# A triangular inversion's input copied in two parts, by two engines: three quarters one pair of heads earlier, one quarter where all of it was

## The chip, the cores and the metric

The kernel runs on one core of a Trainium2 chip. A core has engines that each work through a queue of their own, in order: TensorE (PE: matmuls, and PEld, the loads of their stationary operand), VectorE (DVE), ScalarE (ACT), GpSimd (POOL) and SyncE (SP, which here issues DMA transfers). They meet through semaphores. Data lie in SBUF (128 partitions), matmul results in PSUM. The metric is the device time of one execution in microseconds, as the median of several runs; lower is better. Beside it stands a profile of one execution, in which every instruction has a start, a duration and, where its engine idled, what ended the idle time.

## The reference

Two residual layers over 512 tokens with 1024 features, in float32. Each has a token mixer and a gated ConvFFN. The second layer's mixer is RWKV-7, and its heart is a recurrence over time for 16 heads of 64:

```python
def step(state, inp):
    r_t, w_t, k_t, v_t, a_t, b_t = inp
    sa = jnp.einsum('bhvk,bhk->bhv', state, a_t)
    state = (state * w_t[:, :, None, :]
             + sa[..., None] * b_t[:, :, None, :]
             + v_t[..., None] * k_t[:, :, None, :])
    y_t = jnp.einsum('bhvk,bhk->bhv', state, r_t)
    return state, y_t
```

Around it stand projections of the token-shifted input (r, k, v and low-rank ones for decay, a and gate), a normalization of each head, a bonus term and an output projection. The change touches only how one intermediate of this recurrence is prepared; what is computed stays the same.

## The kernel before

The kernel does the recurrence in chunks of 64 tokens (8 chunks). Within a chunk the steps depend on each other through a 64x64 lower triangular matrix per head and chunk, I minus a strictly triangular part, and the kernel inverts it. Two heads make a **pair**, which fills the 128 partitions; there are 8 pairs, four in each of two **groups** g. The strictly triangular parts of a group lie in the tile `ti[g]` (4 pairs x 8 chunks = 32 units of 64 columns), and the inverse replaces them in place.

`rwkv_main` is made of Python generators. Each `yield` ends a step, and what a step traces goes to the framework.

- `pairs()` is the main line. For pair p it runs `decay` (of pair p + 2: tanh, a scan along time at L911, exponentials, the squares at L913 that the matmul at L923 sums), `operands` (of pair p + 1: products on VectorE) and `products` (of pair p), in three steps. `products` has two halves of four chunks; each multiplies on PE (L973), masks on VectorE (L977, tile `lq`) and lets ScalarE copy the triangular part into `ti` (L978). After the third step p goes into the set `done`. The test runs when the generator is resumed, so a condition such as "3 in done" is first seen after the first step of the next pair.
- `fill` is a chain of generators that keep PE busy: dense projections for k and v (L325 to L327, three matmuls per product: high and low parts), the value path (`value`: L868, L873, L883, L885), then gates and the output projection. `value` uses the PSUM tag `mm`, which has two banks in turn, as the projections do. A bank is free for the next projection when its reader is done; L885 on VectorE is such a reader.
- `invert(g)` is the side line. It takes the two 32x32 diagonal blocks of every 64x64 matrix (`Q`: four sets of 32 partitions and 32 columns) out of `ti[g]` into the tile `ix` (L1041 to L1046), turns every 32x32 block over on VectorE (`turn`, L1051, into tile `li`), sets the diagonal to one (L1055) and then runs a chain of 60 small VectorE instructions (L1062 to L1070), each of which needs the one before. At the end come two more turns (L1051) and matmuls with copies for the block beside the diagonal (L1090 to L1105). For g = 0 the four copies into `ix` are all ScalarE's, of 32 units x 32 columns = 1024 elements each. For g = 1 they are cut already: 24 units on ScalarE, a yield, the last 8 units on VectorE.
- `weave(main, side, fill, rate, lag, side_rate)` interleaves them: per step of the main line so many steps of `fill` and of `side`.

The lines that set where the first inversion starts:

```python
self.weave(until(main, lambda: 3 in done), None, fill, *RATES[0], ktiles=STEPS[0])
inv = invert(0)
for _ in take(inv, FIRST0):
    pass
self.weave(until(main, lambda: KT - 2 in done), inv, fill, *RATES[1], ktiles=STEPS[1])
```

With `FIRST0` = 1, `take` runs `invert(0)` up to its first yield: the copies, the first turn, the diagonal.

The order in an engine's queue is not exactly the order of tracing. The framework plans it when the program is built: among the instructions whose inputs are ready by its own estimate of times it takes the one traced first. A later traced instruction can thus go into a gap that the planner sees. `tc.issue_after(x)` only demands that what is traced under it comes behind x on x's engine. Semaphores follow from the tiles that an instruction reads and writes.

Of the kernel before, what the change touches and what calls it, by code (L numbers as in the profile page):

```python
# [32 lines left out]
RATES = ((1.9, 2), (1.9, 6, 2.2), (0.66, 2, 1.15), (0.72, 2), (1.2, 6, 2.2))  # L33
LEAD = 1
WB = 4
FIRST0, WAIT, STEPS = 1, 1, (2, 2, 2, 2)
# [108 lines left out]
class Emit:  # L145
# [622 lines left out]
    def rwkv_main(self, r, ctx, gain):  # L768
# [22 lines left out]
        ks, used, done, vdone = {}, set(), set(), set()  # L791
# [203 lines left out]
        def pairs():  # L995

            units = [type("Unit", (), {})() for _ in range(KT)]

            def start(p):
                if p >= KT:  # L1000
                    return iter(())
                while p not in ks:
                    next(fill)
                if p == 0:
                    second_factors(p)
                return decay(p, units[p])

            yield from start(0)
            nxt = start(1)
            operands(0, units[0])  # L1010
            for _ in nxt:
                yield
            for p in range(KT):
                nxt = start(p + 2)
                if p + 1 < KT:
                    operands(p + 1, units[p + 1])
                parts = products(p, units[p])
                for n in range(3):
                    next(nxt, None)
                    with ExitStack() as behind:  # L1020
                        if n < 2:
                            behind.enter_context(tc.issue_after(self.last(mybir.EngineType.PE)))
                        next(parts, None)
                    yield
                done.add(p)

        def invert(g):

            tg = ti[g].rearrange("p i c t -> p (i c) t")
            Q = [(slice(64 * hd + 32 * b, 64 * hd + 32 * b + 32), slice(32 * b, 32 * b + 32))
                 for hd in range(2) for b in range(2)]

            def blocks(tag):
                return ip.tile([P, 32, 32], F32, tag=tag, bufs=1 if tag == "off" else 2, name=self.uid(tag))

            x = blocks("ix")
            pr = ip.tile([P, 272], F32, tag="pr", bufs=1, name=self.uid("pr"))
            cut = 24 * g  # L1040
            for us in (slice(0, cut), slice(cut, 32))[1 - g:]:  # L1041
                for rows, cols in Q:
                    if us.start and g == 1:
                        V.tensor_copy(x[rows, us], tg[rows, us, cols])
                    else:
                        S.copy(x[rows, us], tg[rows, us, cols])  # L1046
                if g == 1 and us.start == 0:
                    yield
            def turn(out, src):
                for bs in [slice(n, n + 8) for n in range(0, 32, 8)] if g == 1 else [slice(0, 32)]:  # L1050
                    V.transpose(out[:, bs], src[:, bs])  # L1051

            tt = blocks("li")
            turn(tt.rearrange("p s t -> p t s"), x.rearrange("p u t -> p t u"))
            V.memset(tt.rearrange("p s t -> p (s t)")[:, 0:1024:33], 1.0)  # L1055
            for _ in range(WAIT):
                yield
            for j in range(1, 31):
                ni = 31 - j
                to = tt[:, 0:j, j + 1:32]  # L1060
                if j == 1:
                    V.scalar_tensor_tensor(to[:, 0], tt[:, 1, 2:32], tt[:, 0, 1:2], to[:, 0], ALU.mult, ALU.add)  # L1062
                elif ni == 1:
                    V.scalar_tensor_tensor(to[:, :, 0], tt[:, 0:j, j], tt[:, j, 31:32], to[:, :, 0], ALU.mult, ALU.add)
                else:
                    a = tt[:, j, j + 1:32].unsqueeze(1).to_broadcast([P, j, ni])
                    b = tt[:, 0:j, j].unsqueeze(2).to_broadcast([P, j, ni])
                    q = pr[:, 0:ni * j].rearrange("p (c i) -> p c i", i=ni)
                    V.tensor_tensor(q, a, b, ALU.mult)
                    V.tensor_tensor(to, to, q, ALU.add)  # L1070
                if j % 2 == 1:
                    yield

            z, y = blocks("ix"), blocks("li")
            turn(z.rearrange("p u t -> p t u"), tt)
            if g == 0:
                next(fill)
            turn(y.rearrange("p u t -> p t u"), tt.rearrange("p s t -> p t s"))
            yield
            off, own = blocks("off"), iter(Q)  # L1080
            for i in range(2):
                for hf in range(2):
                    ps = self.acc("aux" if g == 1 else "e").rearrange("p (u t) -> p u t", t=32)
                    us = slice(16 * hf, 16 * hf + 16)
                    for u in range(16):
                        for hd in range(2):
                            b0, b1 = Q[2 * hd][0], Q[2 * hd + 1][0]
                            n = 16 * hf + u
                            if i == 0:
                                nc.tensor.matmul(ps[b1, u, :], tg[b0, n, 32:64], z[b0, n, :], start=True, stop=True,  # L1090
                                                 tile_position=(b0.start, b1.start))
                            else:
                                nc.tensor.matmul(ps[b0, u, :], off[b1, n, :], y[b1, n, :], start=True, stop=True,
                                                 tile_position=(b1.start, b0.start))
                        if u % 8 == 7:
                            if i == 0:
                                rows, cols = next(own)
                                S.copy(tg[rows, :, cols], y[rows])
                            yield
                    for hd in range(2):  # L1100
                        b0, b1 = Q[2 * hd][0], Q[2 * hd + 1][0]
                        if i == 0:
                            S.copy(off[b1, us], ps[b1])
                        else:
                            S.copy(tg[b0, us, 32:64], ps[b0])  # L1105
# [277 lines left out]
        def project():  # L1383

            for g in range(2):
                while g not in gated:
                    yield
                for m in range(2 - 2 * g, KT):
                    if m % 2 == 0:
                        w = wo.take()  # L1390
                    a = self.acc("mm")
                    yield from self.dense_steps(a, w, outs[g], c0=m % 2 * 512)
                    with ExitStack() as behind:
                        if left is None:
                            behind.enter_context(tc.issue_after(self.last(mybir.EngineType.DVE)))
                        V.tensor_tensor(self.h[m], self.h[m], a, ALU.add)
                    if g == 1:
                        self.absorb(m, gain)
# [7 lines left out]
        def take(gen, n):  # L1406
            for _ in range(n):
                if next(gen, self) is self:
                    return
                yield  # L1410

        def until(gen, end):
            for _ in gen:
                yield
                if end():
                    return


        fill = itertools.chain(projections(), gates(), project())
        gw, ga = {}, {}  # L1420
        main = pairs()
        self.weave(until(main, lambda: 3 in done), None, fill, *RATES[0], ktiles=STEPS[0])
        inv = invert(0)
        for _ in take(inv, FIRST0):
            pass
        self.weave(until(main, lambda: KT - 2 in done), inv, fill, *RATES[1], ktiles=STEPS[1])
        load(0, 0)
        ahead = invert(1)
        next(ahead)
        self.weave(main, inv, fill, *RATES[4], ktiles=STEPS[1])  # L1430
# [5 lines left out]
        inv = ahead  # L1436
# [88 lines left out]
```

## Time and profile before

| what | us |
|---|---|
| runs (3) | 1244.2, 1244.65, 1246.1 |
| median | 1244.65 |
| the profiled execution | 1245.55 |
| its span in the profile | 1243.7 |
| first copy into `ix` for group 0 starts (L1046) | 650.96 |
| first turn of group 0 starts (L1051) | 656.56 |
| last small instruction of its chain ends (L1064) | 697.64 |

The difference between the profiled execution's time and its span, 1.85 us, lies outside the profile. Times in rows are from the span's start. A row of the timeline reads: start, duration, engine, line of the source, operation, tile written <- tiles read, shape and count, and in brackets the idle time of the engine before it and what ended that. Durations of neighbours can overlap by some 0.1 us, since an engine starts the next instruction before the last has left it.

### The profile page before, as it was taken

To read this page: it belongs to the slowest core of one execution; us is meant where nothing else is said; L and a number is where in the kernel's file an instruction comes from. 1 tells how busy PE (TensorE), PEld (TensorE's weight loads), DVE (VectorE), ACT (ScalarE), POOL (GpSimd) and SP (SyncE) were. 2 spreads that over 40 slices of the span, in tenths; PEclk is the share of its full clock that TensorE was granted. 3 is DMA by queue.
4 is the path that set the end of the run, shared out by engine and by line. 5 is a ranking of instruction groups with operands and counts; after the bars stand their busy time and mean duration, and the time that the engine had idled before them with its cause. 6 is when DMAs were issued, how large, how long until landed. Compare 5 with 4: busy or idle time off the path is not lost.

```text
span 1243.7 us, 19411 instructions
## 1 busy us (share of the span) xinstructions
PE 1226.8 (99%) x7535; PEld 1000.2 (80%) x7535; DVE 851.1 (68%) x1418; ACT 633.1 (51%) x1089; POOL 81.4 (7%) x106
## 2 busy tenths in 40 slices
PE   9999999999999999999999999999999999999997
PEld 6878888888888888877887777778888888888886
DVE  5566578888876454675899698776777777872323
ACT  6544455555554343466787667424544444543232
POOL 1100200000000001000000013222000000000000
PEclk9999999999999999999999899999999999999999
DMA  7232457887556776326888797654223223333332
GB/s 273 94 105 82 132 180 246 246 249 241 192 172 193 220 226 196 109 81 182 220 242 237 188 280 233 219 171 135 85 102 102 90 97 102 97 88 104 97 93 81
DMA packets 125133, 201.65 MB, mean 162 GB/s; under 512 B 39857, under 2 KB 63153, under 8 KB 125041
## 3 DMA queue, kind: packets, MB, share of 16 engines
q10 hardware_dynamic: 38976, 112.87, 29.5%
q1 hardware_dynamic: 86064, 87.54, 22.6%
q8 instruction: 59, 0.97, 0.3%
q14 instruction: 34, 0.27, 0.1%
HBM read 152.93 MB, written 47.45 MB: 161 GB/s over the span
## 4 chain that ended last, share of the span: by engine, by line
PE 91%; DVE 4%; DMA 3%; ACT 1%; issue 0%; SPq 0%; POOL 0%; DVEq 0%; POOLq 0%; ACTq 0%
PE mm L325 9%; PE mm L327 9%; PE mm L326 9%; PE aux L325 6%; PE aux L326 6%; PE aux L327 6%; PE e L325 6%; PE e L326 6%; PE us L325 6%; PE e L327 6%; PE us L327 6%; PE us L326 6%; PE us L1314 1%; PE aux L973 1%; PE aux L988 1%; PE us L1321 1%
## 5 line engine op out<-in xcount | busy, mean ns | idle before, releaser
L237 ACT CAST w<-w 128x512 fp32r<-128x512 f32 x340 | 206.5, 611 | 359.8 <-PE aux L327 92.6
L238 DVE TENSOR_TENSOR w<-w,w 128x512 fp32r<-128x512 f32 x340 | 230.5, 680 | 180.2 <-ACT w L237 179.6
L325 PE MATMUL mm<-mxh,w 128*128 128x512 f32 x408 | 167.9, 412 | 2.7 <-DVE rt L885 2.6
L327 PE MATMUL mm<-mxh,w 128*128 128x512 f32 x408 | 161.1, 395 | 0.0
L326 PE MATMUL mm<-mxl,w 128*128 128x512 f32 x408 | 160.6, 394 | 0.0
L325 PEld LDWEIGHTS mm<-mxh,w 128*128 128x128 f32 x408 | 77.0, 189 | 22.8 <-DVE rt L885 3.3
L327 PEld LDWEIGHTS mm<-mxh,w 128*128 128x128 f32 x408 | 77.0, 189 | 17.1 <-issue 0.8
L326 PEld LDWEIGHTS mm<-mxl,w 128*128 128x128 f32 x408 | 77.1, 189 | 16.2 <-issue 1.7
L575 ACT ACTIVATE cv<-z,par 128x512 f32<-128x512 f32 x88 | 71.7, 817 | 26.5 <-DVE z L573 21.2
L325 PE MATMUL aux<-mxh,w 128*128 128x512 f32 x216 | 84.5, 391 | 0.0
L325 PE MATMUL us<-mxh,w 128*128 128x512 f32 x216 | 84.5, 391 | 0.0
L327 PE MATMUL aux<-mxh,w 128*128 128x512 f32 x216 | 84.2, 390 | 0.0
L326 PE MATMUL aux<-mxl,w 128*128 128x512 f32 x216 | 84.1, 389 | 0.0
L326 PE MATMUL us<-mxl,w 128*128 128x512 f32 x216 | 84.1, 389 | 0.0
L327 PE MATMUL us<-mxh,w 128*128 128x512 f32 x216 | 84.1, 389 | 0.0
L354 POOL TENSOR_TENSOR ss<-ss,sq 128x512 f32<-128x512 f32 x24 | 31.7, 1323 | 761.1 <-ACT sq L352 761.1
L325 PE MATMUL e<-mxh,w 128*128 128x512 f32 x208 | 81.4, 391 | 0.0
L326 PE MATMUL e<-mxl,w 128*128 128x512 f32 x208 | 81.1, 390 | 0.0
L327 PE MATMUL e<-mxh,w 128*128 128x512 f32 x208 | 81.0, 389 | 0.0
L576 DVE SCALAR_TENSOR_TENSOR cv<-z,par,cv 128x512 f32<-128x512 f32 x88 | 66.0, 752 | 19.5 <-ACT cv L575 19.5
L577 DVE SCALAR_TENSOR_TENSOR cv<-z,par,cv 128x512 f32<-128x512 f32 x88 | 66.0, 752 | 2.9
L325 PEld LDWEIGHTS aux<-mxh,w 128*128 128x128 f32 x216 | 40.5, 188 | 9.0 <-issue 0.5
(1113 smaller groups left out, 2555.2 us busy)
## 6 DMA issues: line engine op xcount, KB each, us to landing
w<-in_wup ACTq DMA_DIRECT2D x88, 512.0 KB, 3.7
w<-in_wdn ACTq DMA_DIRECT2D x32, 512.0 KB, 3.7
st<-std SPq DMA_DIRECT2D x15, 640.0 KB, 6.6
w<-wkd ACTq DMA_DIRECT2D x16, 512.0 KB, 5.1
w<-wvd ACTq DMA_DIRECT2D x16, 512.0 KB, 5.1
w<-wod ACTq DMA_DIRECT2D x16, 512.0 KB, 4.2
w<-in_wdn ACTq DMA_DIRECT2D x16, 384.0 KB, 3.3
w<-in_wsu ACTq DMA_DIRECT2D x8, 512.0 KB, 3.7
```

The costliest lines, as they stand in the source:

```text
L237: nc.scalar.copy(hi[r, :n], src)
L238: (lo_eng or nc.vector).tensor_tensor(lo[r, :n], src, hi[r, :n].bitcast(F32), ALU.subtract)
L325: mm(acc, wh, xh, start=first, stop=False)
L326: mm(acc, wh, xl, start=False, stop=False)
L327: mm(acc, wl, xh, start=False, stop=last)
L354: nc.gpsimd.tensor_tensor(self.ss, self.ss, self.sq, ALU.add)
L575: nc.scalar.activation(c, z[:, 2:], AF.Identity, scale=cw(2, i), bias=self.p("conv_b", l * 44 + i))
L576: nc.vector.scalar_tensor_tensor(c, z[:, 1:T + 1], cw(1, i), c, ALU.mult, ALU.add)
L577: nc.vector.scalar_tensor_tensor(c, z[:, 0:T], cw(0, i), c, ALU.mult, ALU.add)
L973: nc.tensor.matmul(qs[hd][:, c - ch.start, :], bk[H[hd], c, C * hd:C * hd + P], ar[H[hd], c, :], start=True, stop=True)
L988: nc.tensor.matmul(qs[hd][:, c, :], bk[H[hd], c, C * hd:C * hd + P], dg[H[hd], c, :], start=True, stop=True)
L1314: nc.tensor.matmul((us, ux)[hd][H[hd], 1, i, :], ti[g][H[hd], i, c, :], wt[H[hd], i, :], start=True, stop=True)
```

## The change

`invert(g)` cuts its copies for both groups alike: four copies of units 0 to 23 on ScalarE, a yield, four copies of units 24 to 31 on VectorE. The generator `invert(0)` is made before the first `weave`. A wrapper, `opened`, stands around the main line there: at the first step after pair 2 (the third) is done, it runs `invert(0)` up to its new first yield, so that the ScalarE copies of the first three pairs' 24 units are traced behind the first step of pair 3. The call of `take` after the `weave` then runs the step that follows: the VectorE copies of the fourth pair's 8 units, the first turn and the diagonal. Later steps of the inversion are traced where they were.

```diff
-            cut = 24 * g
-            for us in (slice(0, cut), slice(cut, 32))[1 - g:]:
+            for us in (slice(0, 24), slice(24, 32)):
                 for rows, cols in Q:
-                    if us.start and g == 1:
+                    if us.start:
                         V.tensor_copy(x[rows, us], tg[rows, us, cols])
                     else:
                         S.copy(x[rows, us], tg[rows, us, cols])
-                if g == 1 and us.start == 0:
+                if us.start == 0:
                     yield
...
-        self.weave(until(main, lambda: 3 in done), None, fill, *RATES[0], ktiles=STEPS[0])
         inv = invert(0)
+
+        def opened(gen):
+            for _ in gen:
+                if 2 in done and not begun:
+                    begun.append(next(inv))
+                yield
+
+        begun = []
+        self.weave(opened(until(main, lambda: 3 in done)), None, fill, *RATES[0], ktiles=STEPS[0])
         for _ in take(inv, FIRST0):
             pass
```

## The prediction

> **What bounds the kernel now.** I read the page first, for the engine that never rests.
>
> ```profile
> span 1243.7 us, 19411 instructions
> ...
> PE 1226.8 (99%) x7535; PEld 1000.2 (80%) x7535; DVE 851.1 (68%) x1418; ACT 633.1 (51%) x1089; POOL 81.4 (7%) x106
> ```
>
> TensorE (PE) is busy for 1226.8 of 1243.7 us. A change that removes no matmul can win only what PE loses by waiting, 16.9 us in all, and what it loses by running at less than its full clock. So the next view is the busy time of each engine in stretches of 10 us around the code that is changed (columns: busy us and count of PE, weight loads, VectorE (DVE), ScalarE (ACT), GpSimd; then the granted PE clock, DMA share, GB/s).
>
> ```profile
> 630.00:640.00 10.00, 10.00 (x57) 8.09 (x56) 9.94 (x18) 7.86 (x15) 0.00 (x0) 1.00 0.66 182
> 640.00:650.00 10.00, 10.00 (x107) 8.46 (x106) 8.80 (x17) 7.49 (x16) 0.11 (x1) 1.00 0.80 236
> 650.00:660.00 10.00, 9.34 (x66) 7.74 (x68) 7.06 (x16) 8.71 (x14) 0.00 (x0) 1.00 0.89 238
> 660.00:670.00 10.00, 9.44 (x82) 7.37 (x81) 9.93 (x22) 7.68 (x15) 0.11 (x1) 1.00 0.79 206
> 670.00:680.00 10.00, 10.00 (x98) 8.61 (x98) 9.93 (x25) 7.32 (x17) 0.00 (x0) 1.00 0.93 246
> 680.00:690.00 10.00, 9.65 (x82) 7.51 (x82) 9.76 (x23) 4.51 (x10) 0.61 (x2) 1.00 1.03 283
> 690.00:700.00 10.00, 7.53 (x48) 5.43 (x48) 9.52 (x24) 4.21 (x8) 0.00 (x0) 0.90 0.87 246
> 700.00:710.00 10.00, 10.00 (x133) 8.09 (x129) 3.15 (x4) 6.17 (x11) 0.00 (x0) 0.76 0.39 105
> ```
>
> Three things are to be seen. Up to 650 PE is never idle. From 660 to 700 VectorE is, at 9.5 to 9.9 of 10, so in that stage it is as much the bound as PE is. And PE pays twice near 695: it idles for 2.47 us in 690 to 700, and the granted clock falls to 0.90 and then 0.76, which is 1.0 + 2.4 = 3.4 us of full-speed work lost. The view of what PE waited for, 650 to 700, names the waits:
>
> ```profile
> PE mm L325 <- DVE rt L885: 2.6, 2, 2.3
> PE e L923 <- ACT sq L913: 0.7, 1, 0.7
> PE e L899 <- DVE kn L950: 0.6, 1, 0.6
> ```
>
> One wait is on ScalarE (0.7 us), the rest on a late VectorE. Why VectorE is late shows where the first inversion begins. The timeline of ScalarE, then that of VectorE:
>
> ```profile
> 650.96 1.04 ACT L1046 COPY ix<-ti 32x1024 f32<-32x1024 f32 x1
> 652.01 0.62 ACT L957 COPY bk<-bk 64x512 f32<-64x512 f32 x1
> 652.63 1.05 ACT L1046 COPY ix<-ti 32x1024 f32<-32x1024 f32 x1
> 653.70 0.41 ACT L978 COPY ti<-lq 64x256 f32<-64x256 f32 x1
> 654.12 1.04 ACT L1046 COPY ix<-ti 32x1024 f32<-32x1024 f32 x1
> 655.07 0.40 ACT L978 COPY ti<-lq 64x256 f32<-64x256 f32 x1
> 655.48 1.05 ACT L1046 COPY ix<-ti 32x1024 f32<-32x1024 f32 x1
> 656.55 0.63 ACT L913 ACTIVATE sq<-kn 128x512 f32<-128x512 f32 x1
> ```
>
> ```profile
> 652.57 1.22 DVE L911 TENSOR_TENSOR_SCAN sq<-cst,sq 128x512 f32<-128x512 f32 x1
> 656.56 2.02 DVE L1051 STREAM_TRANSPOSE li<-ix 128x1024 f32<-128x1024 f32 x1 [2.77 <-ACT ix L1046]
> ```
>
> VectorE stands at the transpose for 2.77 us until the fourth copy is done; the same copies hold L913 back, for which PE waits. The four copies were traced one after another, yet other instructions stand between them: the order in a queue is the framework's plan and not that of the source. I come back to this.
>
> **The change part by part.** It splits the four copies of 1024 elements into four of 768 on ScalarE, traced after the first half of the fourth pair, and four of 256 on VectorE where all four stood. The second inversion (g = 1) already has this form, so the trace has both prices. VectorE's row and ScalarE's:
>
> ```profile
> 714.75 1.18 DVE L1044 COPY ix<-ti 32x256 f32<-32x256 f32 x4
> ```
>
> ```profile
> 711.77 2.51 ACT L1046 COPY ix<-ti 32x768 f32<-32x768 f32 x3
> ```
>
> *VectorE.* It gains the 2.77 us of waiting and pays 1.18 us for four copies. They come in behind the scan that ends at 652.57 + 1.22 = 653.79, so the transpose would begin near 654.97 and not at 656.56: **1.6 us earlier**. Two reasons could make it less. The instructions behind the transpose wait for L923, which gets only 0.7 us earlier; the copies could also be planned into VectorE's idle time before, which would make it more (at most 2.77).
>
> *ScalarE before 650.* Three copies take 2.51 us, so four take 2.51 / 3 x 4 = 3.3 us. Their last input is the third pair's second half, and from 630 to 650 ScalarE idles 2.14 + 2.51 = 4.65 us by the table above. This holds them, but in pieces:
>
> ```profile
> ACT sq L906 <- PE e L901: 1.7, 1, 1.7
> ACT mt L690 <- DVE mxl L238: 1.0, 1, 1.0
> ```
>
> (That view is ScalarE's waits from 628 to 650, the two longest.) Only these two pieces hold a copy of 0.84 us whole. What queues behind a misplaced copy is the pair's own chain, above all the square L913 that PE's L923 reads. Its slack there:
>
> ```profile
> 640.05 0.63 ACT L913 ACTIVATE sq<-kn 128x512 f32<-128x512 f32 x1
> ```
>
> ```profile
> 641.64 1.05 PE L923 MATMUL e<-cst,sq 128*128 128x128 f32 x8
> ```
>
> L913 ends at 640.68, 0.96 us before PE wants it. One copy ahead of it costs nothing; two cost 2 x 0.84 - 0.96 = 0.7 us of PE; four would cost 2.4 us. I take nothing, because PE has 10.00 of 10 busy there with filling matmuls and 1.7 us of the gaps lie behind L913; 0 to 2.4 us goes into the range.
>
> *ScalarE after 650.* 4.2 us of copies go away, so L913 is no longer held and PE's 0.67 us before L923 go. No DMA, PSUM bank or SP instruction is added, and ScalarE's weight loads (issued from its queue) move with it by about a microsecond at most, none of which PE is seen to wait for here. The number of steps per turn of the interleaving loop is unchanged, since one extra step is used up early.
>
> *The sum.* From 656.56 to 697 VectorE is busy for 9.5 to 9.9 of every 10 us and waits for no other engine for long, so if its order stays, everything it does there is 1.6 us earlier, and so is the end of PE's last wait. The two timelines at this place (PE, then VectorE):
>
> ```profile
> 692.30 1.02 PE L883 MATMUL mm<-rt,wb 128*128 128x512 f32 x2
> ...
> 696.99 0.50 PE L325 MATMUL mm<-mxh,w 128*128 128x512 f32 x1 [2.28 <-DVE rt L885]
> ```
>
> ```profile
> 696.25 0.68 DVE L885 TENSOR_TENSOR rt<-mm,v 128x512 f32<-128x512 f32 x1
> ...
> 697.67 1.99 DVE L1051 STREAM_TRANSPOSE ix<-li 128x1024 f32<-128x1024 f32 x1
> 699.51 1.97 DVE L1051 STREAM_TRANSPOSE li<-li 128x1024 f32<-128x1024 f32 x1
> ```
>
> PE's small waits are used up first: 0.67 (gone with the copies), 0.6 (L950) and about 0.3 (the other L885, 2.6 - 2.3) make 1.6 us. PE thus arrives at the last wait 1.6 us earlier, VectorE's L885 comes 1.6 us earlier too, and the wait stays about **2.2 us** long. With it stays the clock's fall behind it. What is late next is the same L885. So the gain is 1.6 us and not 1.6 + 2.28 + 3.4. Behind 700 PE is the bound again and carries the shift on. Against the profiled execution's own 1245.55 us (span 1243.7 and 1.85 around it) this gives 1243.95; the median of the runs is 0.9 lower, 1244.65, and from it the forecast is 1244.65 - 1.6 = **1243.05 us**.
>
> [...]
>
> **The rivals.**
>
> *The clock's fall goes too.* If the planner puts L885 before some of the small chain instructions that now precede it (L883 ends at 693.3, L885 starts only at 696.25), or if PE and VectorE shift so that the wait is cut, the 2.2 us shrink and the clock may stay at full speed. Beside it, PE waited 0.7 and 0.6 us in 650 to 670 at a clock of 1.00, so short waits do no harm. It gives 1.6 + 3.4 = 5.0 us: 1244.65 - 5.0 = 1239.65. For it: 2.28 us is the only wait in the stage with this effect. Against: nothing in the change touches L885's place. [...]
>
> *L885 behind the transposes (slower).* The inversion's chain now begins 1.6 us earlier, PE's own work only 0.7 us, and only 697.67 - 696.85 = 0.8 us of chain lies between L885's end and the first of the two transposes of 2 us. If the plan moves the chain ahead by more than 0.8 us against L885, L885 is queued behind one transpose or both. Without L885 before it the first transpose starts at 697.67 - 1.6 - 0.6 = 695.5; it holds L885 until 697.3 and the second (699.51 - 697.67 = 1.84 each) until 699.2. PE then goes on at 698.1 or 699.9, not 696.99: 1.1 or 2.9 us slower, 1245.75 or 1247.55, with the clock's fall as before. It decides from 0.8 us on.
>
> *Given back on ScalarE.* The copies fall before L913 in the earlier pair, PE waits there for 0.7 to 2.4 us, and VectorE's gain is paid for: 1243.75 to 1245.45.
>
> *It doesn't do what it says.* The plan could put the early copies no earlier than 650. ScalarE then does 3.3 in place of 4.2 us beside VectorE's 1.18: 0.9 us won, 1243.75.
>
> **How the numbers follow.** About 0.2%, 2.5 us, is what a measurement of this kernel can tell from no change. Chances: forecast 0.38 (0.05 of it beyond 2.5 us of gain, by VectorE's copies going into idle time), the clock's fall gone 0.30, L885 behind the transposes 0.22 (0.06 behind one, which is within 0.2%; 0.16 behind both), given back or not done 0.10 (0.04 of it slower, by four copies ahead of L913 and nothing won on VectorE: 1244.65 + 2.4 = 1247.05 and a little more). Faster: 0.05 + 0.30 = 0.35. Slower: 0.16 + 0.04 = 0.20. Same: 0.33 + 0.06 + 0.06 = 0.45. The range takes in the rival with the clock and nearly all of both transposes: 1239.0 to 1247.5; the likeliest case alone would be 1241.9 (all 2.77 us) to 1244.7 (nothing kept).
>
> **What would show it.** In the profile after: L1046 with 768 elements between 628 and 650 and L1044 eight times; the transpose L1051 near 655 with no wait; no wait of PE at the L923 near 657; no wait of PE near 641. The wait at L325 for L885 ends near 695.3 and is still over 2 us, and 690 to 710 still shows two clocks below 1.00. If the clock there is 1.00, the first rival holds; if L885 starts behind a transpose, the second. The forecast is wrong if the plan of the queues differs in the scan stage (730 to 850) as well, which nothing here bounds.

## The result, and the profile after

The changed kernel takes 1252.93 us (median of 4 runs, 1251.29 to 1253.23). The kernel before, run beside it on the same chip, takes 1244.43 (4 runs, 1243.8 to 1246.1). The ratio is 1.0062, 95% interval 1.0049 to 1.0076: **slower by 0.6%**, 7.7 us (0.0062 x 1244.43; the two medians lie 8.5 us apart), and outside the predicted range. The profiled execution after took 1253.23 us.

In `invert` and the scan, line numbers after are one lower than before from L1044 on: the copies on VectorE are L1043, those on ScalarE L1045, the turn is L1050.

The page of the changed kernel, its span and TensorE's row:

```profile
span 1251.4 us, 19418 instructions
...
PE 1229.0 (98%) x7535; PEld 1001.6 (80%) x7535; DVE 853.0 (68%) x1422; ACT 631.2 (50%) x1089; POOL 82.2 (7%) x106
```

The span is 7.7 us longer, and PE is busy only 2.2 us longer (1229.0 - 1226.8). So PE does no more work; it waits 5.5 us more, and a part of its work runs at a lower clock. The windows of 10 us, with the columns of the prediction's table, show two of the places:

```profile
640.00:650.00 10.00, 9.00 (x90) 7.65 (x89) 8.54 (x15) 8.80 (x18) 0.11 (x1) 1.00 0.83 241
...
690.00:700.00 10.00, 7.31 (x65) 5.50 (x63) 9.49 (x23) 6.21 (x14) 0.00 (x0) 1.00 0.87 222
700.00:710.00 10.00, 7.99 (x52) 6.41 (x53) 1.96 (x2) 4.56 (x9) 0.00 (x0) 0.50 0.20 65
```

In 640 to 650, where PE was busy for 10.00 us before, it now idles for 1.0. In 690 to 710 it idles for 4.7 us where it idled for 2.5, and the clock falls to 0.50. The view of PE's waits from 600 to 850 names these and a third place (total us, times, longest):

```profile
PE mm L325 <- DVE rt L885: 5.0, 2, 4.7
PE us L1313 <- DVE wt L1303: 2.6, 3, 1.4
PE e L923 <- ACT sq L913: 1.6, 2, 1.0
PE us L1320 <- ACT vu L1315: 1.2, 1, 1.2
```

The second and the fourth row belong to the scan of the chunks behind 725: L1313 waits for VectorE's L1303, L1320 for ScalarE's copy L1315.

**First place, 641.** ScalarE's timeline shows where the early copies of 768 elements went, and what stands behind them:

```profile
631.12 1.68 ACT L1045 COPY ix<-ti 32x768 f32<-32x768 f32 x2
...
634.10 0.83 ACT L1045 COPY ix<-ti 32x768 f32<-32x768 f32 x1
...
638.13 0.83 ACT L1045 COPY ix<-ti 32x768 f32<-32x768 f32 x1
...
642.98 0.63 ACT L913 ACTIVATE sq<-kn 128x512 f32<-128x512 f32 x1
```

All four stand ahead of the square L913, which began at 640.05 before. PE's timeline has the answer to it:

```profile
643.66 1.16 PE L923 MATMUL e<-cst,sq 128*128 128x128 f32 x8 [1.00 <-ACT sq L913]
```

**Second place, 700.** VectorE's timeline at the start of the inversion, and at the end of its chain:

```profile
650.27 1.17 DVE L1043 COPY ix<-ti 32x256 f32<-32x256 f32 x4
651.48 2.08 DVE L1050 STREAM_TRANSPOSE li<-ix 128x1024 f32<-128x1024 f32 x1
653.43 0.65 DVE L951 SCALAR_TENSOR_TENSOR ta<-ta,rb 128x512 f32<-128x512 f32 x1
...
657.97 1.19 DVE L911 TENSOR_TENSOR_SCAN sq<-cst,sq 128x512 f32<-128x512 f32 x1
...
659.08 0.23 DVE L1061 SCALAR_TENSOR_TENSOR li<-li 128x30 f32<-128x30 f32 x1
...
697.72 1.92 DVE L1050 STREAM_TRANSPOSE ix<-li 128x1024 f32<-128x1024 f32 x1
699.50 1.94 DVE L1050 STREAM_TRANSPOSE li<-li 128x1024 f32<-128x1024 f32 x1
701.26 0.70 DVE L885 TENSOR_TENSOR rt<-mm,v 128x512 f32<-128x512 f32 x1
```

The change does what it says: the first turn starts at 651.48, 5.1 us earlier than before, and waits for nothing. But the plan put copies and turn ahead of the products L951 to L955 and the scan L911, and the first instruction of the chain, L1061, still stands behind L911. It starts at 659.08; before, it was 658.66:

```profile
658.66 0.21 DVE L1062 SCALAR_TENSOR_TENSOR li<-li 128x30 f32<-128x30 f32 x1
```

So the 5.1 us at the turn do not reach the chain. At the other end L885 was planned before the last short instructions of the chain; now it stands behind both turns. PE goes on here:

```profile
702.01 0.79 PE L325 MATMUL mm<-mxh,w 128*128 128x512 f32 x1 [4.71 <-DVE rt L885]
```

**Third place, 768.** ScalarE before:

```profile
757.57 0.37 ACT L1316 COPY vu<-us 64x256 f32<-64x256 f32 x1 [1.13 <-PE us L1314]
758.61 1.50 ACT L873 COPY vt<-aux 64x256 f32<-64x256 f32 x4 [0.67 <-PE aux L868]
```

and after:

```profile
764.26 1.04 ACT L1097 COPY ti<-li 32x1024 f32<-32x1024 f32 x1 [1.23 <-DVE li L1050]
765.32 1.50 ACT L873 COPY vt<-aux 64x256 f32<-64x256 f32 x4
766.72 0.72 ACT L1113 ACTIVATE sq<-h,par 128x512 f32<-128x512 f32 x1
767.47 0.37 ACT L1315 COPY vu<-us 64x256 f32<-64x256 f32 x1
```

The copy `vu`, which PE's L1320 reads, stood ahead of L873. Now it stands behind it, behind L1113 and behind a copy-back of the second inversion (L1097) that itself waits 1.23 us for VectorE. The change touches none of these lines.

**The ledger.** I compare when PE starts the same matmul in two traces; the difference is the **lag** to the trace of before. Six marks: the L923 that starts at 623.5 before (the entry, ahead of the change), the next L923 (641.64), the L883 at 692.30, those at 721.97 and 750.80, and a matmul of the last ConvFFN (L327 at 1204.99). All times are those of the rows, each from its own span's start. What stands at the entry arises ahead of the change, at the start and near 588 us, and scatters from 0.2 to 2.1 us between the kernels here, although their code is the same up to there; it is taken off. The first column is the lag at the entry, the others are the lag since then, in us (where two queues of PE differ, a mark can be off by some tenths):

| kernel | entry | 641 | 692 | 722 | 751 | 1205 |
|---|---|---|---|---|---|---|
| after | 0.86 | 1.15 | 1.74 | 4.69 | 5.73 | 6.88 |
| e1 | 0.53 | 0.00 | -0.71 | -0.99 | 1.86 | 4.49 |
| e2 | 1.10 | 1.16 | 0.49 | 2.39 | 6.37 | 11.71 |
| e3 | 0.25 | 1.15 | 1.77 | -2.30 | -1.87 | 2.15 |
| e4 | 0.95 | 0.00 | 1.32 | 4.25 | 5.31 | 6.50 |
| e5 | 1.53 | 0.18 | 2.95 | 2.94 | 5.52 | 6.73 |
| e6 | 0.86 | 0.29 | -0.75 | -3.00 | -2.81 | -2.76 |
| e7 | 2.08 | 0.00 | -1.54 | -1.40 | -1.34 | -1.21 |
| e8 | 1.21 | 0.00 | -1.50 | -2.19 | -2.17 | -2.16 |
| e9 | 0.86 | 0.01 | -1.52 | -2.55 | -3.34 | -3.30 |
| e10 | 0.23 | 0.00 | -0.03 | -2.22 | -1.95 | -1.96 |
| e11 | 0.86 | 1.15 | 1.77 | 5.00 | 5.01 | 5.05 |

For the changed kernel: 1.15 us at L913's square, 0.6 more up to 692, 2.95 around 700, 2.2 in the scan behind 722. These 6.88 us and the 0.86 at the entry make the 7.7 us by which the span is longer.

### The profile page after: what moved, and what is told of

The parts are those of the page before. It is cut to its first block, busy times and chain, and to the rows that moved or that the text cites. A ratio compares the mean times of both kernels' runs of the same rounds, so it can differ in the third digit from the quotient of the medians.

```text
span 1251.4 us, 19418 instructions
## 1 busy us (share of the span) xinstructions
PE 1229.0 (98%) x7535; PEld 1001.6 (80%) x7535; DVE 853.0 (68%) x1422; ACT 631.2 (50%) x1089; POOL 82.2 (7%) x106
## 5 line engine op out<-in xcount | busy, mean ns | idle before, releaser
L325 PE MATMUL mm<-mxh,w 128*128 128x512 f32 x408 | 168.9, 414 | 5.4 <-DVE rt L885 5.0
L327 PE MATMUL mm<-mxh,w 128*128 128x512 f32 x408 | 161.3, 395 | 0.0
L325 PEld LDWEIGHTS mm<-mxh,w 128*128 128x128 f32 x408 | 77.4, 190 | 25.9 <-DVE rt L885 5.7
L327 PEld LDWEIGHTS mm<-mxh,w 128*128 128x128 f32 x408 | 77.2, 189 | 17.1 <-issue 0.8
L325 PE MATMUL aux<-mxh,w 128*128 128x512 f32 x216 | 84.6, 392 | 0.0
L325 PE MATMUL us<-mxh,w 128*128 128x512 f32 x216 | 84.6, 392 | 0.0
L327 PE MATMUL aux<-mxh,w 128*128 128x512 f32 x216 | 84.3, 390 | 0.0
L327 PE MATMUL us<-mxh,w 128*128 128x512 f32 x216 | 84.2, 390 | 0.0
L325 PE MATMUL e<-mxh,w 128*128 128x512 f32 x208 | 81.5, 392 | 0.0
L327 PE MATMUL e<-mxh,w 128*128 128x512 f32 x208 | 81.1, 390 | 0.0
L238 DVE TENSOR_TENSOR pwl<-pw,pwh 128x512 fp32r<-128x512 f32 (+1 forms) x51 | 34.8, 682 | 20.4 <-DMA wod<-pwl 6.3
```

The costliest lines, as they stand in the source:

```text
L238: (lo_eng or nc.vector).tensor_tensor(lo[r, :n], src, hi[r, :n].bitcast(F32), ALU.subtract)
L325: mm(acc, wh, xh, start=first, stop=False)
L327: mm(acc, wl, xh, start=False, stop=last)
```

## The experiments

The first four change the source. Two theories stood at the start: **Q**, the loss is L885 behind the turns in VectorE's queue; **S**, it is ScalarE's early copies ahead of the square. Each ratio is against runs of the kernel before on the same chip.

### e1: the copies cut, but not moved

```diff
         inv = invert(0)
-        def opened(gen): ...
+        next(inv)
```

> The copies are cut 24/8 between ScalarE and VectorE, but all of them stand where the four ScalarE copies stood before; none is early. In VectorE's queue L885 of the third value tile stands between the two turns at the chain's end (before: ahead of both; after: behind both). Theory Q (the loss is L885's place behind the turns): PE waits for it about 1.9 us longer than in the kernel before, and the clock falls as before: 1245.5 to 1248. Theory S (the loss is the early ScalarE copies, which starve the main line near 640): without them no loss, 1243 to 1245.

1252.0 us, ratio 1.0056 [1.0038, 1.0074]. Both missed. The first inversion even gains (lag -0.99 at 722); VectorE's timeline shows L885 behind one turn and not both:

```profile
695.78 1.92 DVE L1050 STREAM_TRANSPOSE ix<-li 128x1024 f32<-128x1024 f32 x1
697.54 0.68 DVE L885 TENSOR_TENSOR rt<-mm,v 128x512 f32<-128x512 f32 x1
698.13 2.15 DVE L1050 STREAM_TRANSPOSE li<-li 128x1024 f32<-128x1024 f32 x1
```

All of the loss, 5.5 us (4.49 + 0.99), comes behind 722, in a stage in which no line was edited. PE waits there for L1315 (2.5 us, once), for L1303 (2.1) and for L854 (1.2), and the granted clock is 0.84 in 730 to 740, which is 1.6 us of full-speed work. Neither theory knows this place.

### e2: the early part alone

The changed kernel, with the last 8 units copied by ScalarE as well, where the fourth pair is done.

```diff
-                    if us.start:
+                    if us.start and g == 1:
                         V.tensor_copy(x[rows, us], tg[rows, us, cols])
```

> The 24 units are copied early by ScalarE, the last 8 at the old place by ScalarE too, none by VectorE. L885 stands between the two turns. Theory Q: a loss of one turn (1.9 us) and of the wait near 641 (about 1.2 us): 1246.5 to 1249. Theory S: the whole loss of the changed kernel, 1251 to 1253.

1253.45 us, ratio 1.0072 [1.0047, 1.0097]: as slow as the whole change. Both ranges missed, S by 0.45 us; the ledger shows that the loss is not at S's place. The same 1.16 us at the square, then 1.9 around 700 and 9.3 in the scan stage. The profiled execution (1258.23) is the slowest of its runs, with three falls of the clock in it (granted 0.988 on the whole), so the 9.3 is not typical of the kernel.

### e3: both turns behind L885

```diff
-            turn(z.rearrange("p u t -> p t u"), tt)
+            with ExitStack() as behind:
+                if g == 0:
+                    behind.enter_context(tc.issue_after(bonus))
+                turn(z.rearrange("p u t -> p t u"), tt)
```

(the second turn alike; `bonus` is L885 of the third value tile.)

> The changed kernel, but the two turns at the chain's end are ordered behind L885 of the third value tile. Theory Q: L885 starts near 698 in place of 701.3, PE waits 1 to 1.5 us there in place of 4.7, and the clock falls less or not at all: 1245 to 1249. Theory S: at most 1 us better than the changed kernel, 1251.5 to 1253.

1248.68 us, ratio 1.003 [1.0018, 1.0042]. Q's number. PE's wait for L885 is 1.0 us instead of 4.7, and the clock stays whole, as the window shows:

```profile
700.00:710.00 10.00, 10.00 (x140) 7.97 (x133) 3.53 (x4) 8.15 (x14) 0.00 (x0) 1.00 0.64 173
```

At 722 this kernel is 2.30 us ahead of before, and then it loses 4.45 us in the scan stage, 1.7 of them by a fall of the clock (0.83 in 760 to 770). PE's timeline (line numbers 8 higher here):

```profile
761.12 0.69 PE L1328 MATMUL us<-vu,cbt 128*64 128x64 f32 x16 [2.52 <-ACT vu L1323]
```

So Q is right about its place, and there is another place that it does not explain.

### e4: the early copies behind the square

```diff
-                if 2 in done and not begun:
-                    begun.append(next(inv))
+                if 5 in r.square and not begun:
+                    with tc.issue_after(r.square[5]):
+                        begun.append(next(inv))
```

> The changed kernel, but the early ScalarE copies are ordered behind the square L913 for which PE waits near 641. L885 stays behind both turns. Theory Q: only the wait near 641 goes (1.2 us), 1250.5 to 1252. Theory S: most of the loss goes, 1244 to 1247.

1253.07 us, ratio 1.0065 [1.005, 1.0081]. Both ranges missed, Q by 1.1 us and S by 6. The 1.15 us at 641 are gone (lag 0.00), PE waits 0.9 us at a later L923 instead, and all the rest is as in the changed kernel. So the total does not fall, and S is at most a sixth of the loss (1.15 of 6.88).

### A third theory: the plan of the queues

All four lose behind 722, by 2.2 to 9.3 us, through instructions that no edit touches (in e1, e2 and e3 partly by further falls of the clock). Laid beside each other, the programs of before and after have the same instructions in the same order of tracing but for the copies. The order in the queues differs in one stretch: some 130 places of ScalarE's queue, some 200 of VectorE's, some 300 of PE's, 12 of SyncE's, from about 630 us to the end of the second inversion. So theory **P**: the time is lost by the new order that the framework plans, and not by the work of the copies. Rival **W**: the added and moved work itself delays the main line.

To tell them apart, the next kernels write the order of each queue out by hand. `HOLD` lists, for each engine, the numbers of its instructions in order of tracing; a dependency without a semaphore keeps neighbours in that order.

```diff
+def hold(tc):
...
+    for eng, text in HOLD.items():
...
+        for a, b in zip(order, order[1:]):
+            tc.add_manual_dep(traced[eng][b], traced[eng][a].name,
+                              mybir.DependencyInfo(mybir.DependencyClass.NoSync, mybir.DependencyReason.DATA), reason="hold")
```

### e5: the new order, the old work

The kernel before with `HOLD` of the order after. Two places differ from it: ScalarE's four copies stand near their old place, at 652.89 to 657.09, and the first turn stands behind them, right ahead of the scan L911 (at 657.12 and 659.16 in the trace, and not behind L911, as the expectation has it).

> The kernel before in all its work, its copies too (one block of 32 on ScalarE), with the queues of ScalarE, VectorE, TensorE and SyncE in the order that the changed kernel has around the inversions; the first block's turn alone stays behind L911, and ScalarE's copies stay before it. Theory P (the loss comes from the new order of the queues): 1248.5 to 1252 us, with the waits of the scan stage (TensorE for L885's, L1304's and L1316's copies) as in the changed kernel. Theory W (the loss comes from the added and moved copies themselves): 1243.5 to 1246.

1253.68 us, ratio 1.0071 [1.0056, 1.0086]. This is above P's range by 1.7 us and far above W's: **no copy was cut or given to another engine, and a loss as large as the change's is there.** So the added and moved work is not needed for it. Its waits:

```profile
PE mm L325 <- DVE rt L885: 4.0, 1, 4.0
PE e L923 <- ACT sq L913: 2.7, 1, 2.7
PE us L1314 <- DVE wt L1304: 2.6, 3, 1.4
PE us L1321 <- ACT vu L1316: 1.2, 1, 1.2
```

The scan stage has the waits of after (the same 2.6 and 1.2), and it loses 3.8 us in place of 2.2, because the clock falls there once more (0.83 in 730 to 740, 1.7 us). The first inversion is another case than after: the old copies stand ahead of L913 of a later pair while PE already has the new order, PE waits 2.7 us there, and the 2.95 us at 692 come from this mixture, which is neither kernel's. At 700 the lag does not grow (4.0 us of wait, but only 1.7 us lost to the clock, 0.83 in 700 to 710, make up the 2.3 + 3.4 of before). So e5 shows the size of what an order can cost and the waits of the scan stage; it does not repeat the changed kernel place by place.

### e6 and e7: the new work, the old order

The changed kernel with `HOLD` of the order before. In e6 ScalarE's copies stand where the plan put them after (ahead of L913 of the sixth pair), in e7 behind that square, two and two from 649.47 to 654.85. That is close to the old place and not a pair of heads earlier, so e7 tests the cut more than the early start. VectorE's four copies stand right ahead of the turn, behind L911.

> The changed kernel's copies at the places that they have in the changed kernel on ScalarE (ahead of the square L913 of the sixth pair), VectorE's copies right ahead of the first turn behind L911, and every other instruction of the four queues in the order of the kernel before. Theory P: 1243 to 1246 us: up to 1.2 us late at the square, 1.6 us earlier at L885, nothing lost in the scan stage. Theory W: 1249 to 1253, as the changed kernel, since the same work is done at the same early place.

> As the one before, but ScalarE's copies two and two behind the square of the sixth pair, where the trace of before shows ScalarE idle between the rows of L905 and L957. Theory P: 1242 to 1244 us: nothing lost at the square, the turn 1.6 us earlier, L885 with it; if the wait for L885 falls so far that the clock is not halved near 700, 1239 to 1241. Theory W: 1246 or more.

e6: 1243.38 us, ratio 0.9994 [0.9983, 1.0005]. e7: 1243.84, ratio 0.999 [0.9979, 1.0]. P; W is refuted: the same work that takes 1252.93 us in the planned order takes 1243.4 to 1243.8 in this one. Both intervals reach 1.0, so neither kernel is clearly faster than the one before. In the scan stage both lose 0.2 us or nothing. At L325 the row of e6:

```profile
697.11 0.50 PE L325 MATMUL mm<-mxh,w 128*128 128x512 f32 x1 [2.30 <-DVE rt L885]
```

and that of e7:

```profile
697.54 0.51 PE L325 MATMUL mm<-mxh,w 128*128 128x512 f32 x1 [2.29 <-DVE rt L885]
```

Less the lag at the entry, PE goes on at 695.46 in e7 (697.54 - 2.08) and at 696.25 in e6 (697.11 - 0.86), against 696.99 before: 1.5 and 0.7 us earlier, with the wait as long as it was. The 0.8 between them is the price of the early place on ScalarE. The windows tell what became of it; e6:

```profile
700.00:710.00 10.00, 10.00 (x144) 7.87 (x139) 3.65 (x4) 8.09 (x14) 0.00 (x0) 1.00 0.50 138
```

and e7:

```profile
700.00:710.00 10.00, 9.73 (x133) 8.00 (x133) 3.36 (x4) 5.46 (x10) 0.00 (x0) 0.71 0.38 108
```

The same wait of 2.3 us left the clock whole in one profiled execution and halved it in the other.

### e8: L885 ahead of the last ten short instructions

e7 with number 802 of VectorE's list (L885) moved ahead of number 790 (the multiplication L1068 of 128x150).

> As the one before, and the third value tile's copy L885 moved ahead of the last ten short instructions of VectorE's chain (ahead of L1069's 128x150). Theory P, with the clock's fall due to the wait for L885: TensorE's wait of 2.28 us goes, and the 3.4 us that the half clock costs: 1237.5 to 1240.5 us. If the clock falls all the same: 1241 to 1243. Theory W: 1246 or more.

1245.29 us, ratio 1.0002 [0.9993, 1.0011]: all three missed, W by less than a microsecond and for another reason, since the lag is -2.16 and not above 0. L885 runs at once, and PE's wait goes to the next reader of the inversion. PE's timeline:

```profile
699.43 0.69 PE L1089 MATMUL e<-ix,ti 32*32 32x32 f32 x32 [2.71 <-DVE ix L1050]
```

So L885 had been the first in line, but the stage is bound by VectorE's chain, whose turn PE needs next. And the clock still falls: in all ten runs of e8 the granted clock is 0.994 to 0.997, while in five of the ten runs of e7 it is 0.998 or 0.999.

### e9 and e10: and the inversion's first matmuls later

In PE's list the first 16 source matmuls of L1089 (32 records) go behind the rest of L868 and ten of L325. e9 is this on e8; e10 is this and the early L885 on the kernel **before**, with its own copies.

> The kernel of the run before (changed copies, order of before, L885 early) with one more move: the first 16 source matmuls of L1089 (the 32 records at 699.43 there) stand on TensorE behind the rest of L868 and ten matmuls of L325 that do not need the inversion. Theory (TensorE's wait of 2.71 us there is for the first of the two turns, and nothing but the order makes it): the wait goes, 2.7 us, and if the clock then stays at 1.00 another 2.5 to 3.4: 1239 to 1242.5 us. Rival (VectorE's chain sets the stage, whatever stands on TensorE): the wait comes back at the next reader of the inversion or of VectorE, 1244 to 1246.

> The kernel before with its own copies and its own order, and only the two moves: L885 ahead of the last ten short instructions of the chain, and the first 16 source matmuls of L1089 behind the rest of L868 and ten of L325. Theory: TensorE's 2.28 us for L885 go, and the clock's fall with them if nothing else waits as long: 1239 to 1242.5. If the earlier copies of the change are needed to make room (they bring the chain 1.6 us forward): 1242.5 to 1244. Rival: 1244 to 1246.

e9: 1242.2 us, ratio 0.9979 [0.997, 0.9988]: faster than the kernel before by 2.6 us (0.0021 x 1245.23), and so than the changed one. The wait at 699 is gone; the first L1089 now follows the matmuls ahead of it without idle time:

```profile
699.30 0.69 PE L1089 MATMUL e<-ix,ti 32*32 32x32 f32 x32
```

A part of it comes back behind it, as the rival said; the longest of e9's waits is new, and another new one of 0.8 us stands at L883:

```profile
PE e L1092 <- ACT off L1102: 1.4, 1, 1.4
```

In the profiled executions e9 ends 1.1 us ahead of e8 (-3.30 against -2.16), not the 2.7 of the wait. e10: 1243.8 us, ratio 0.9993 [0.9985, 1.0002]: in the band that was given for "the earlier copies are needed". e9 less e10 is what the change itself, in the form that it has in e7, is worth under one and the same order: 1.6 us by the medians, 1.3 by the ledger. The two intervals overlap a little, so this size is an indication. Up to 692 the ledger of e10 is that of before (-0.03), so writing the order out by `HOLD` costs nothing by itself there.

### e11: the old order in the scan stage alone

The changed kernel with its own order up to the end of the first chain, and the order of before from there on.

> The changed kernel in its own order up to the end of the first inversion's chain (VectorE up to L885 of the third value tile, ScalarE up to the third of the second inversion's copies), and from there on in the order of the kernel before. Theory P with two sites: the 5 us lost up to 708 stay and the 2 us lost between 730 and 766 go: 1249.5 to 1251.5 us. If the loss of the scan stage comes from the lateness of the first stage and not from the order there: 1252 to 1254.

1250.57 us, ratio 1.0046 [1.0033, 1.0059]: P with two sites. Up to 722 the ledger is that of the changed kernel (5.00 against 4.69); behind it nothing is added (5.05 at the end, against 6.88). Its waits from 700 on:

```profile
PE mm L325 <- DVE rt L885: 4.7, 1, 4.7
PE us L1313 <- DVE wt L1303: 1.0, 2, 0.8
```

L1313 is back at the 1.0 us of before, and the wait for L1315 is gone. So the loss of the scan stage isn't an echo of the first stage's lateness; it is the order there.

## Why the prediction was wrong

- **What bounds the kernel** was right: PE, and in 660 to 700 VectorE with it. e8 sharpens it: not L885 but the chain with its turns is what PE waits for.
- **VectorE, "1.6 us earlier"**, rests on the words "if its order stays". This is the step that failed. With the order of before the number is right: in e7 the turn starts at 657.04, which less the 2.08 at the entry is 654.96, as predicted (654.97), PE goes on 1.5 us earlier, and e9 less e10 gives 1.3 to 1.6. With the planned order the turn starts 5.1 us earlier by the rows, but the chain's first instruction 0.4 us later (0.4 us earlier, if the 0.86 at the entry is taken off), and L885 falls behind both turns.
- **"Nothing in the change touches L885's place"** was wrong in the same way. The second rival described what happened: PE was to go on at 699.9 and to lose 2.9 us. It went on at 701.15 (702.01 less the 0.86 at the entry) and lost 2.95 between 692 and 722. The place was right; that the price came out so close is partly luck, since the rival has the chain 1.6 us earlier and the clock's fall as before, and the trace shows a chain 0.4 us earlier and a longer fall. The chance (0.16) was too small: the planner orders by its own estimate of times, so any edit upstream may move an instruction that nobody edits. The rival's total of 1247.55 is too low mainly because it has only this one site.
- **The clock "as before"**: before was at half clock for 6.8 us (twice the 1.0 + 2.4), the changed kernel for about 10 (the windows show 0.50 in 700 to 710). But its half clock began while PE still waited for L885: PE is busy for 1.48 of the first 3.42 us (last section). So it lost about 4.15 us of full-speed work, before 3.3. These 0.8 us and the 2.2 us more of idle time (4.7 against 2.5) make 3.1, near the 2.95 of the ledger. Where the wait is 4.7 us (after, e4, e11) the fall was longer in all three (10.2 to 10.4 us).
- **ScalarE's copies, "I take nothing"**: 1.15 us at the square. All four copies went ahead of L913, a case that the prediction priced at 2.4; the plan also took other work from between, and PE waited 1.00 us. The bound of 0 to 2.4 held, the value taken did not. Here too the order has a part: in e6 all four stand ahead of the square as well, and it loses 0.3 us there and 0.8 up to L885.
- **PE's 0.67 us at 657, "gone with the copies"**, did not go. The copies no longer hold L913 back, but the early turn holds VectorE's L952 back, for which ScalarE waits ahead of L913. ScalarE's timeline after:

```profile
655.31 0.62 ACT L957 COPY bk<-bk 64x512 f32<-64x512 f32 x1 [2.00 <-DVE bk L952]
...
655.95 0.63 ACT L913 ACTIVATE sq<-kn 128x512 f32<-128x512 f32 x1
```

PE's timeline, with this wait and a new one:

```profile
656.64 1.16 PE L923 MATMUL e<-cst,sq 128*128 128x128 f32 x8 [0.55 <-ACT sq L913]
...
664.71 1.16 PE L868 MATMUL mm<-cst,v 128*128 128x128 f32 x8 [0.81 <-ACT v L854]
```

One wait took the place of another: 0.55 us in place of 0.67, and 0.81 at L868, which before did not have, in place of the 0.6 at L899, which is gone.

- **The scan stage**, "which nothing here bounds", cost 2.2 us (6.88 - 4.69; by e11 against after, 2.4 by the medians). It was named, and had no price and no chance. From the range's top of 1247.5, this and the square's 1.15 make more than half of what is missing.

The sum as measured, by the ledger: 1.15 (square) + 0.6 (up to 692) + 2.95 (L885 and clock) + 2.2 (scan) = 6.9 us, beside 0.9 at the entry that is not the change's. The 0.6 is not explained: between these two marks PE waits for about 1.7 us in both kernels.

What stays open: why the planner, given slightly different copies, chose this order. The runs show that the order costs the time; its estimates are not in a trace. Open too is which of the four queues carries the loss, since `HOLD` set all four at once. e1 shows that cutting the copies, without moving them, is enough to change the scan stage.

## What to carry to other kernels

Where a framework plans the queues, an edit is two changes: the work, and a new plan for all that follows. Time them apart, by holding the order of before around the new work and the new order around the old work; here the work was worth about 1.5 us (an indication), and the plan cost about 9 (0.0071 x 1245 in e5; 1252.93 against 1243.4 to 1243.8 in e6 and e7). And when a wait is to be removed, look for the next reader of the same late engine (L1089 behind L885) before counting the wait as a gain.

## What was not expected of the hardware

The fall of PE's clock does not follow from the length of a wait alone. The time at half clock in 690 to 720, as twice the sum of 10 us x (1 - granted clock) over the three windows of each profile, is: none in e3, e6 and e10, 3.4 us in e1, e5, e8 and e9, 6.8 to 7.0 in before and e7, 10.2 to 10.4 in after, e2, e4 and e11. These are steps of about 3.4 us. Yet a wait of 2.30 us was followed by none in e6 and one of 2.29 by 7.0 us in e7, and the waits of 3.8 and 4.0 us in e1 and e5 were followed by 3.4 us, less than the 6.8 us behind the 2.28 of before.

The traces also show what goes with a fall. The granted clock that the trace of before records falls at 697.97 us, for 6.827 us, and that of after at 700.08, for 10.240: two and three times 3.413 us. The record's first entry, at full clock, begins at 5.06 us in before and at 7.17 in after. From there to the fall both traces have 692.906 us, which is 203 times 3.4133, although the fall comes 2.1 us later in after. So I lay stretches of this length from the first entry on; that the fall keeps to them in the other kernels too is an estimate from these two traces. In e7, whose first entry lies at 9.39 us, the stretch that ends with the fall is this:

```profile
695.46:698.88 3.42, 1.34 (x6) 1.12 (x7) 3.18 (x10) 1.84 (x5) 0.00 (x0) 1.00 0.85 226
```

In e6 (first entry at 7.01 us) the same wait falls into two stretches:

```profile
693.08:696.50 3.42, 1.73 (x7) 0.94 (x5) 3.22 (x11) 1.97 (x5) 0.00 (x0) 1.00 0.84 188
696.50:699.91 3.41, 1.95 (x12) 1.50 (x14) 3.31 (x6) 1.93 (x3) 0.00 (x0) 1.00 0.80 231
```

PE idles for 2.1 us of the one, for 1.7 and 1.5 us of the other two (the 1.5 with a later wait). The stretch that ends with the fall has 2.28 us of idle time in before and 2.77 in after:

```profile
694.56:697.97 3.41, 1.13 (x5) 0.85 (x5) 3.13 (x12) 1.83 (x4) 0.00 (x0) 1.00 0.92 239
```

```profile
696.66:700.08 3.42, 0.65 (x3) 0.19 (x1) 3.37 (x5) 3.33 (x6) 0.00 (x0) 1.00 0.96 245
```

Up to 1195 us no other stretch at full clock has more than 0.9 us in before and 1.2 in after, and no other fall follows there. The two traces also differ behind the fall. In before PE idles for 0.2 us of the first stretch at half clock, and the fall lasts two stretches; in after it idles for 1.9 us of it, and the fall lasts three:

```profile
697.97:701.38 3.41, 3.22 (x40) 2.60 (x40) 3.41 (x2) 0.92 (x2) 0.00 (x0) 0.50 0.47 154
```

```profile
700.07:703.49 3.42, 1.48 (x4) 1.19 (x5) 1.89 (x2) 2.42 (x4) 0.00 (x0) 0.50 0.12 37
```

From which idle time on the clock falls, and what sets how long, is not shown by these traces.

A single profile therefore says little about a change that only shortens such a wait: between e6 and e7, with the same wait, lies a fall that costs about 3.2 us of full-speed work. Runs of one kernel differ in this too. Of the 57 runs of the kernel before that stand beside the experiments, 34 have a granted clock of 0.996 or 0.997 and 23 of 0.998 or 0.999; the latter are 1.4 us shorter on average. That is less than the 3.3 us of work that the fall takes in the profile of before, and the runs do not show why.
